# Expert loop of a mixture layer: gathers ahead of scatters, tables two chunks sooner, turned tiles one per chunk, bias rows alternating, spare rows from the last tile

## The chip, the cores and the metric

The kernel runs on one core of a Trainium2 chip (trn2). The metric is the device time of one execution in microseconds; less is better. The profile comes from one execution of the same program, recorded by the hardware profiler; its times count from the first instruction of the span.

## The reference, cut to what matters

One decoder layer over 512 tokens of width 1024. A mixing sublayer (pooling and short convolution, then an output projection) and a layer norm give `x1`. A mixture of 32 experts follows, of which each token uses 4. A second norm, a gated embedding and a third norm make the output.

```python
x = layer_norm(ALPHA * x + mix, ln1_g, ln1_b)
# for each expert e, on the rows that chose it:
gu = xb @ w_gate_up[e] + b_gate_up[e]
gate = minimum(gu[:, :1024], 7.0); up = clip(gu[:, 1024:], -7.0, 7.0)
y = ((up + 1.0) * gate * sigmoid(1.702 * gate)) @ w_down[e] + b_down[e]
# weighted by the token's softmaxed router logits and summed over its 4 experts
x = layer_norm(ALPHA * x + ffn, ln2_g, ln2_b)
x = layer_norm(ALPHA * x + sigmoid(x @ ple_gate_w + ple_gate_b) * (p @ ple_proj), ln3_g, ln3_b)
```

## The kernel before, in words

**Precision.** Every float32 matrix is divided into a high part (rounded by a copy on ScalarE, L114) and a low part (the rest, a subtraction on VectorE, L117, called the split here); a product is three matrix products, `mm3`, L210 to L212. Weights are streamed once, in chunks of 1 MB, through a ring of buffers: `load` (L102), `split`, and `ahead(j)`, which gives a used chunk's buffers back and splits what is due three to five chunks ahead.

**First part.** The input projection and the mixers fill `y`. `project(i)` multiplies token tile i (128 tokens) by the output weights, 48 products; `norm(i)` adds the residual in `x1[i]` on VectorE (`piece`, L274), takes a power on GpSimd (L291), and scales (L296, L298). `x1[i]` is loaded from `x` by GpSimd's DMA (L509). Both `x1d` (rows to gather) and `acc` (rows to scatter-add into) are written from it (L551). `acc` has 96 spare rows behind the 512, into which an expert's unused places scatter; L518 fills them once with finite numbers, from rows of a tile of `x1` before the norm overwrites it. `turn(i)` transposes the normed tile on TensorE (L307) for the router; `turn(0)` stands three products into `project(2)`.

**Expert loop (L897).** Each expert has 96 places for rows (a loop at the end handles any more). In the order of the program, expert e does:
1. four bias products of 64 rows (L903), the two halves of gate on the array's rows 0 to 63, the two of up on 64 to 127;
2. eight chunks of gate/up weights, k = 0 to 7, each 12 products, then `ahead`. At k = 2 the hidden rows of expert e - 1 are transposed (`split_t`, L307, L322, L323). In even experts (and in expert 1) `tables` makes for two experts the lists of rows and their weights: at k = 1 and 2 a one-hot table on VectorE (L614), at k = 6 eight narrow products (L640) and their decoding (L621 to L628);
3. the transposition of the rows gathered for expert e + 1;
4. `act`: L335 on VectorE, L338 on ScalarE, L339 on GpSimd, the sigmoid L344, the multiply L345 on GpSimd, L347 on VectorE;
5. the down projection of expert e - 1, four chunks j = 0 to 3, with the multiply L345 queued behind j = 0 and L347 behind j = 2, then `emit`: L354 scales on ScalarE and L355 scatters on GpSimd (a DMA that adds);
6. `gather_next`: an indirect DMA on GpSimd (L313) fetches the rows of expert e + 2 into the buffer that the sigmoid has left.

All transpositions and tables share two PSUM banks (`tr`), taken in turn; a bank is free when its result has been read. Expert 0 has no down projection; it also holds `weigh` and, after k = 5, the transposition for expert 1 (TURN1). Expert 5 runs `further` (lists for experts with more than 96 rows). Expert 19 (EMBED + 1) runs `embed_parts`: four tiles of `p` are transposed (L841) and divided (L843), one at each of k = 2 to 5. Expert 31 runs `prepare`: the four gate tables are transposed (L893) all at k = 2. The order on every queue is the order of the program text (`manual_schedule`).

Of the kernel before, what the change touches and what calls it, by code (L numbers as in the profile page):

```python
# [21 lines left out]
S = 512  # L22
NT = S // P
D = 1024
ND = D // P
E = 32
TOPK = 4
F = 1024
CAP = 96
# [19 lines left out]
def tile_layer(ctx: ExitStack, tc: tile.TileContext, x, p, w_in, pool_mix, pool_scale, conv_w, w_out,  # L49
               ln1_g, ln1_b, router_w, router_b, w_gate_up, b_gate_up, w_down, b_down,  # L50
               ln2_g, ln2_b, ple_proj, ple_gate_w, ple_gate_b, ln3_g, ln3_b, out):
    nc = tc.nc
# [8 lines left out]
    def at(name, b, dtype, n=2048, offset=0):  # L61

        return nc.alloc_sbuf_tensor_at(name, [P, n], dtype, offset=base0 + 8192 * b + 4 * offset).ap()
# [4 lines left out]
    acc = dram.tile([S + CAP, D], F32, name="acc")  # L68

    def big(n=P):  # L70
        return ps.tile([n, 2, 512], F32, tag="big", name="big", bufs=3)

    def tr(shape):
        return ps.tile(shape, F32, tag="tr", name="tr", bufs=2)
# [75 lines left out]
    def done(j, queue=nc.sync):  # L150

        give(*owned.pop(j))
        used[0] = j + 1
        fill(queue)
# [11 lines left out]
    def ahead(j):  # L166
        done(j)
        splits()
# [39 lines left out]
    def mm3(o, ah, al, bh, bl, start, stop):  # L208

        nc.tensor.matmul(o, ah, bl, start=start, stop=False)  # L210
        nc.tensor.matmul(o, al, bh, start=False, stop=False)  # L211
        nc.tensor.matmul(o, ah, bh, start=False, stop=stop)  # L212
# [98 lines left out]
    def gather(e):  # L311
        xg = mp2.tile([P, F], F32, tag="sg", name="xg")[:CAP]
        nc.gpsimd.indirect_dma_start(out=xg, out_offset=None, in_=x1d,  # L313
                                     in_offset=bass.IndirectOffsetOnAxis(ap=idxg[:, e:e + 1], axis=0))
        return xg
# [10 lines left out]
    def split_t(src, tag, pool, bufs):  # L326
        both, put = two_parts(tag, pool, bufs)
        transposed(src, CAP, put)
        return both
# [19 lines left out]
    def emit(o, gate, idx, y, halves=False):  # L349
        if halves:  # L350
            nc.scalar.activation(y[:, :512], o[:, 0], AF.Copy, scale=gate)
            nc.vector.tensor_scalar(y[:, 512:], o[:, 1], gate, None, op0=ALU.mult)
        else:
            nc.scalar.activation(y, o.rearrange("p a b -> p (a b)"), AF.Copy, scale=gate)  # L354
        nc.gpsimd.indirect_dma_start(out=acc, out_offset=bass.IndirectOffsetOnAxis(ap=idx, axis=0), in_=y,  # L355
                                     in_offset=None, compute_op=ALU.add)
# [9 lines left out]
    with tc.tile_pool(name="mix", bufs=1, side=RIGHT) as q:  # L366
# [112 lines left out]
        for j, cs in zip(order_in, c_in):  # L479
            o = o1 if len(cs) == 2 else big()  # L480
# [22 lines left out]
    x1 = [mp2.tile([P, D], F32, tag=n, name="x1") for n in ("gm", "h")]  # L503
# [11 lines left out]
        nc.scalar.dma_start(braw[32 * k:32 * k + 32], b_gate_up[0, :, (k // 2) * F:(k // 2 + 1) * F])  # L515
    nc.scalar.dma_start(rw, router_w[0].rearrange("(k p) e -> p k e", p=P))
    nc.scalar.dma_start(rb, router_b.to_broadcast([P, E]))
    nc.gpsimd.dma_start(acc[S:, :], x1[0][:CAP])  # L518
    lv = cp.tile([P, NT, E + 8], F32, name="lv")
    gsp = cp.tile([P, NT, 3, E], F32R, name="gsp")  # L520
    m8 = cp.tile([P, NT, 2, 8], F32, name="m8")
# [337 lines left out]
    def down(e, after={}, before={}):  # L859
        ah, al = hT.pop(e)  # L860
        o = big(CAP)
        for j in range(4):
            wh, wl = parts.pop(c_dn[e][j])
            for n in range(2):
                ns = slice(n * 512, (n + 1) * 512)
                for b in range(2):
                    k = 2 * j + b
                    mm3(o[:, n], ah[:, k], al[:, k], wh[:, b, ns], wl[:, b, ns], k == 0, k == ND - 1)
            for f in before.get(j, ()):
                f()  # L870
            if e == E - 2 and j == 2:
                done(c_dn[e][j])
            elif e < E - 1 or j < 3:
                ahead(c_dn[e][j])
            for f in after.get(j, ()):
                f()
        emit(o, gs[:, e:e + 1], idxs[:, e:e + 1], yos[e % 2][:CAP], e == E - 1)
        if e == E - 1:
            done(c_dn[e][-1])
# [6 lines left out]
    def prepare():  # L886

        nc.scalar.copy(bd, b3[:96])
        nc.vector.tensor_sub(bd[64:], b3[64:96], bd[64:].bitcast(F32))
        yield  # L890
        for i in range(NT):
            gt = tr([96, P])
            nc.tensor.transpose(gt, gsp[:, i].rearrange("p a b -> p (a b)").bitcast(F32), ident)  # L893
            nc.scalar.copy(gt_[:96, i * P:(i + 1) * P], gt)

    steps = iter(())
    for e in range(E):  # L897
        ah, al = xT.pop(e)
        gp, up = big(CAP), big(CAP)
        halves = [(gp, 0, 0), (gp, 1, 512), (up, 0, 1024), (up, 1, 1536)]  # L900
        for o, n, c in halves:
            r = slice(64 * (c // F), 64 * (c // F) + 64)
            nc.tensor.matmul(o[:, n], sel[r, e:e + 1].to_broadcast([64, CAP]), bsp[r, c % F:c % F + 512],  # L903
                             start=True, stop=False)
        for k in range(ND):
            wh, wl = parts.pop(c_gu[e][k])
            for o, n, c in halves:
                cs = slice(c, c + 512)
                mm3(o[:, n], ah[:, k], al[:, k], wh[:, 0, cs], wl[:, 0, cs], False, k == ND - 1)
            if k < ND - 1 or e:  # L910
                ahead(c_gu[e][k])
            if e == 0 and k == 0:
                next(first1, None)
                xg[1] = gather(1)
            if e == 0 and k == 1:
                weigh()
            if e == 0 and k == TURN1:
                xT[1] = split_t(xg.pop(1), "x", mp1, 1)
            if e and k == 2:
                hT[e - 1] = split_t(hs.pop(e - 1), "h", mp2, 1)  # L920
            if k == 1:
                steps = (tables(2, mp1) if e == 0 else tables(0, mp1) if e == 1 else
                         tables(e + 2, mp1) if e % 2 == 0 and e + 2 < E else
                         further() if e == 5 else prepare() if e == E - 1 else iter(()))
            if k in (1, 2, 6):
                next(steps, None)
            if e == EMBED + 1:
                if k == 1:
                    embed_steps = embed_parts()
                if 1 <= k <= 6:  # L930
                    next(embed_steps, None)
        last = e == E - 1
        if e and not last:
            xT[e + 1] = split_t(xg.pop(e + 1), "x", mp1, 1)
        steps_h = act(gp, up, lambda n: mp2.tile([P, F], F32, tag=n, name=n)[:CAP], nc.vector if last else nc.gpsimd)
        hs[e] = next(steps_h)
        if not last:
            next(steps_h)
        if e == 0:
            ahead(c_gu[0][-1])  # L940

        def multiply(steps_h=steps_h):
            next(steps_h)

        def gather_next(e=e):
            if e + 2 < E:
                xg[e + 2] = gather(e + 2)

        def finish(steps_h=steps_h):
            next(steps_h, None)  # L950

        if last:
            down(e - 1, {0: [finish, finish, finish]}, {3: [last_turn]})
            limit[0] = len(chunks)
            fill(nc.gpsimd)
        elif e:
            down(e - 1, {0: [multiply], 2: [finish]})
            gather_next()
        else:
            multiply()  # L960
            gather_next()
            finish()
        if e == EMBED - 1:

            spare_tiles = [more2.tile([P, 2, D], F32, tag=f"m{k}", name="after") for k in range(4)]
            ple = [t[:, k] for t in spare_tiles[:2] for k in range(2)]
            g2, b2 = spare_tiles[2][:, 0], spare_tiles[2][:, 1]
            pt, graw = spare_tiles[3][:, 0].rearrange("p (a b) -> p a b", a=NT), spare_tiles[3][:64, 1]
            assert len(late) == NT - 2 and len(extra) == 4
            pgb = at("pgb", RING + 1, F32R, D)[:64]  # L970
            ph, pl = (at(f"p{k}", RING + 2, F32R, D, k * D).rearrange("p (i k t) -> p i k t", i=NT, k=2) for k in range(2))
            nc.gpsimd.memset(graw, 0.0)
            nc.gpsimd.dma_start(pt, p[0, 0].rearrange("(i p) c -> p i c", p=P))

            for h in (0, 32):
                nc.gpsimd.dma_start(graw[h:h + 1], ple_gate_b)
            nc.gpsimd.dma_start(g2, ln2_g.to_broadcast([P, D]))
            nc.gpsimd.dma_start(b2, ln2_b.to_broadcast([P, D]))
        if e == EMBED + 1:
            embed()  # L980
            g3, b3 = spare_tiles[3][:, 0], spare_tiles[3][:, 1]
            gt_ = at("gt", RING + 2, F32R, S)
            bd = at("bd", RING + 1, F32R, D, D)[:96]

            for k in range(3):
                nc.gpsimd.dma_start(b3[32 * k:32 * k + 32], b_down[0])
# [124 lines left out]
```

## Time and profile before

| | |
|---|---|
| median of 3 runs | 1450.96 us (1449.4 to 1452.47) |
| the profiled execution | 1454.03 us |
| its span, mean granted clock | 1452.2 us, 0.989 |
| ScalarE busy | 952.4 us, 66% |
| GpSimd busy | 521.1 us, 36% |
| moved by DMA | 464.43 MB, mean 320 GB/s |

In the rows further down, PE is TensorE's products, PEld its weight loads, DVE is VectorE, ACT ScalarE, POOL GpSimd. A row names the line, the operation, what is written from what, and in brackets how long the engine stood idle just before and what ended that ("issue": nothing that the profile shows). The granted clock is the share of 2.4 GHz that TensorE got.

### The profile page before, as it was taken

The page shows a single profiled execution, that of the slowest core. Times are in us where ns is not written, and L with a number is a line of the kernel's source. Part 1 is how long each engine was busy: PE and PEld are TensorE (multiplying, and loading weights), DVE is VectorE, ACT ScalarE, POOL GpSimd, SP SyncE. Part 2 cuts the span into 40 slices and gives each one's busy share as a digit, 9 for nine tenths or more (in the row PEclk, how much of TensorE's full clock was granted, in tenths as well). Part 3 has the DMA queues.
Part 4 walks back from the last instruction along what each step waited for, and adds up shares of the span by engine and source line. Part 5 has one row for each costly group of instructions (what it writes and reads, how often), then busy time and mean ns, then how long its engine had stood idle before and what let it go on. Part 6 is the DMA issues. An engine that isn't in the chain of part 4 may idle for free. (4 is left out here: it accounts for less than half of the span.)

```text
span 1452.2 us, 17680 instructions
## 1 busy us (share of the span) xinstructions
PE 1404.6 (97%) x6630; PEld 1003.2 (69%) x6630; DVE 1236.7 (85%) x1049; ACT 952.4 (66%) x741; POOL 521.1 (36%) x203
## 2 busy tenths in 40 slices
PE   9999999999999999999999998999999999998896
PEld 8787766766666666767666666766666666665575
DVE  7645589999999999999989997799999999997785
ACT  5321267777777777777777776677777777776631
POOL 1101025455345555555543351134343434331100
PEclk9999999999999999999999999999999999999998
DMA  9326889999999999999889999899999999998321
GB/s 332 110 88 219 330 327 340 384 376 365 366 375 374 364 371 353 377 362 354 318 281 373 361 397 336 298 346 385 365 382 358 381 364 377 370 378 302 108 102 44
DMA packets 98071, 464.43 MB, mean 320 GB/s; under 512 B 9424, under 2 KB 19168, under 8 KB 65216
## 3 DMA queue, kind: packets, MB, share of 16 engines
q1 hardware_dynamic: 86240, 426.02, 76.7%
q0 software_dynamic: 10080, 35.53, 9.8%
q10 hardware_dynamic: 1664, 1.72, 0.5%
q8 instruction: 54, 0.88, 0.2%
q14 instruction: 33, 0.27, 0.1%
HBM read 443.97 MB, written 19.27 MB: 319 GB/s over the span
## 5 line engine op out<-in xcount | busy, mean ns | idle before, releaser
L355 POOL DMA_INDIRECT acc<-yo,idxs x32 | 200.9, 6277 | 187.1 <-ACT yo L354 181.8
L339 POOL TENSOR_SCALAR h<-h 96x1024 f32<-96x1024 f32 x31 | 40.9, 1318 | 428.4 <-ACT h L338 428.4
L212 PE MATMUL big<-chunk,xh 128*96 128x512 f32 x480 | 189.1, 394 | 0.0
L211 PE MATMUL big<-chunk,xl 128*96 128x512 f32 x480 | 189.0, 394 | 0.0
L313 POOL DMA_INDIRECT xg<-x1d,idxg x31 | 142.4, 4595 | 22.8 <-DVE idxg L653 13.7
L345 POOL TENSOR_TENSOR gm<-gm,sg 96x1024 f32<-96x1024 f32 x31 | 103.5, 3337 | 66.4 <-ACT sg L344 64.0
L211 PE MATMUL big<-chunk,hl 128*96 128x512 f32 x268 | 106.2, 396 | 0.0
L212 PE MATMUL big<-chunk,hh 128*96 128x512 f32 x268 | 105.6, 394 | 0.0
L212 PEld LDWEIGHTS big<-chunk,xh 128*96 128x96 f32 x480 | 77.5, 161 | 33.1
L211 PEld LDWEIGHTS big<-chunk,xl 128*96 128x96 f32 x480 | 77.7, 162 | 30.6
L212 PEld LDWEIGHTS big<-chunk,hh 128*96 128x96 f32 x268 | 43.4, 162 | 19.0
L211 PEld LDWEIGHTS big<-chunk,hl 128*96 128x96 f32 x268 | 43.3, 162 | 17.6
L322 ACT CAST xh<-tr 128x384 fp32r<-128x384 f32 x64 | 27.4, 478 | 34.8 <-PE tr L307 34.8
L291 POOL TENSOR_TENSOR mv<-mv,mhalf 128x1 f32<-128x1 f32 x12 | 7.9, 655 | 109.5 <-DVE mv L290 97.8
L344 ACT ACTIVATE sg<-gm 96x1024 f32<-96x1024 f32 x32 | 34.0, 1062 | 16.2 <-DVE gm L335 9.4
L117 DVE TENSOR_TENSOR ring2dt.float32r<-ring2dt.float,ring13dt.float32r 128x2048 fp32r<-128x2048 f32 x14 | 34.7, 2482 | 9.4 <-ACT ring13dt.float32r L114 9.4
L354 ACT ACTIVATE yo<-big,gs 96x1024 f32<-96x1024 f32 x31 | 34.4, 1110 | 10.8 <-PE big L212 10.8
L347 DVE SCALAR_TENSOR_TENSOR h<-h,gm 96x1024 f32<-96x1024 f32 x32 | 38.8, 1211 | 2.6 <-POOL gm L345 2.6
L117 DVE TENSOR_TENSOR ring5dt.float32r<-ring5dt.float,ring3dt.float32r 128x2048 fp32r<-128x2048 f32 x13 | 31.1, 2392 | 11.0 <-ACT ring3dt.float32r L114 11.0
L117 DVE TENSOR_TENSOR ring12dt.float32r<-ring12dt.float,ring6dt.float32r 128x2048 fp32r<-128x2048 f32 x14 | 32.6, 2327 | 8.4 <-ACT ring6dt.float32r L114 8.4
L335 DVE TENSOR_SCALAR gm<-big 96x1024 f32<-96x1024 f32 x32 | 38.7, 1211 | 0.0
L117 DVE TENSOR_TENSOR ring10dt.float32r<-ring10dt.float,ring12dt.float32r 128x2048 fp32r<-128x2048 f32 x14 | 34.7, 2482 | 4.4 <-ACT ring12dt.float32r L114 4.2
(577 smaller groups left out, 4474.2 us busy)
## 6 DMA issues: line engine op xcount, KB each, us to landing
ring10dt.float<-in_w_gate_up_dram SPq DMA_DIRECT2D x18, 1024.0 KB, 6.7
ring2dt.float<-in_w_gate_up_dram SPq DMA_DIRECT2D x18, 1024.0 KB, 7.5
ring3dt.float<-in_w_gate_up_dram SPq DMA_DIRECT2D x18, 1024.0 KB, 7.6
ring4dt.float<-in_w_gate_up_dram SPq DMA_DIRECT2D x18, 1024.0 KB, 7.5
ring9dt.float<-in_w_gate_up_dram SPq DMA_DIRECT2D x18, 1024.0 KB, 8.0
ring13dt.float<-in_w_gate_up_dram SPq DMA_DIRECT2D x17, 1024.0 KB, 6.8
ring1dt.float<-in_w_gate_up_dram SPq DMA_DIRECT2D x17, 1024.0 KB, 6.5
ring5dt.float<-in_w_gate_up_dram SPq DMA_DIRECT2D x17, 1024.0 KB, 6.9
```

The lines of the kernel that those rows point to most:

```text
L117: second()
L211: nc.tensor.matmul(o, al, bh, start=False, stop=False)
L212: nc.tensor.matmul(o, ah, bh, start=False, stop=stop)
L313: nc.gpsimd.indirect_dma_start(out=xg, out_offset=None, in_=x1d, in_offset=bass.IndirectOffsetOnAxis(ap=idxg[:, e:e + 1], axis=0))
L322: nc.scalar.copy(hi[:, 4 * h:4 * h + 4], t)
L335: nc.vector.tensor_scalar(gm, gp, LIMIT, None, op0=ALU.min)
L339: mul.tensor_scalar(h, h, LIMIT, -LIMIT, op0=ALU.min, op1=ALU.max)
L344: nc.scalar.activation(sg, gm, AF.Sigmoid, scale=SW_ALPHA)
L345: mul.tensor_mul(gm, gm, sg)
L347: nc.vector.scalar_tensor_tensor(h, h, 1.0, gm, op0=ALU.add, op1=ALU.mult)
L354: nc.scalar.activation(y, o.rearrange("p a b -> p (a b)"), AF.Copy, scale=gate)
L355: nc.gpsimd.indirect_dma_start(out=acc, out_offset=bass.IndirectOffsetOnAxis(ap=idx, axis=0), in_=y, in_offset=None, compute_op=ALU.add)
```

## The change

The spare rows are filled from tile 3 in place of tile 0. `prepare` yields before each tile, so that it does one tile per step. The bias products go gate half 0, up half 0, gate half 1, up half 1. The third step of `tables` and `further` runs at k = 4 in place of 6; the steps of `prepare` run at k = 1, 3, 4, 5, 6, and those of `embed_parts` too, in place of 1 to 6 (of which the last had nothing left to do). From expert 1 on the gather for expert e + 2 is queued behind chunk j = 1 of the down projection, ahead of the scatter.

```diff
--- before.py
+++ after.py
@@ -515,7 +515,7 @@
         nc.scalar.dma_start(braw[32 * k:32 * k + 32], b_gate_up[0, :, (k // 2) * F:(k // 2 + 1) * F])
     nc.scalar.dma_start(rw, router_w[0].rearrange("(k p) e -> p k e", p=P))
     nc.scalar.dma_start(rb, router_b.to_broadcast([P, E]))
-    nc.gpsimd.dma_start(acc[S:, :], x1[0][:CAP])
+    nc.gpsimd.dma_start(acc[S:, :], x1[NT - 1][:CAP])
     lv = cp.tile([P, NT, E + 8], F32, name="lv")
     gsp = cp.tile([P, NT, 3, E], F32R, name="gsp")
     m8 = cp.tile([P, NT, 2, 8], F32, name="m8")
@@ -887,8 +887,8 @@
 
         nc.scalar.copy(bd, b3[:96])
         nc.vector.tensor_sub(bd[64:], b3[64:96], bd[64:].bitcast(F32))
-        yield
         for i in range(NT):
+            yield
             gt = tr([96, P])
             nc.tensor.transpose(gt, gsp[:, i].rearrange("p a b -> p (a b)").bitcast(F32), ident)
             nc.scalar.copy(gt_[:96, i * P:(i + 1) * P], gt)
@@ -898,7 +898,7 @@
         ah, al = xT.pop(e)
         gp, up = big(CAP), big(CAP)
         halves = [(gp, 0, 0), (gp, 1, 512), (up, 0, 1024), (up, 1, 1536)]
-        for o, n, c in halves:
+        for o, n, c in halves[::2] + halves[1::2]:
             r = slice(64 * (c // F), 64 * (c // F) + 64)
             nc.tensor.matmul(o[:, n], sel[r, e:e + 1].to_broadcast([64, CAP]), bsp[r, c % F:c % F + 512],
                              start=True, stop=False)
@@ -922,12 +922,12 @@
                 steps = (tables(2, mp1) if e == 0 else tables(0, mp1) if e == 1 else
                          tables(e + 2, mp1) if e % 2 == 0 and e + 2 < E else
                          further() if e == 5 else prepare() if e == E - 1 else iter(()))
-            if k in (1, 2, 6):
+            if k in ((1, 2, 4) if e < E - 1 else (1, 3, 4, 5, 6)):
                 next(steps, None)
             if e == EMBED + 1:
                 if k == 1:
                     embed_steps = embed_parts()
-                if 1 <= k <= 6:
+                if k in (1, 3, 4, 5, 6):
                     next(embed_steps, None)
         last = e == E - 1
         if e and not last:
@@ -954,8 +954,7 @@
             limit[0] = len(chunks)
             fill(nc.gpsimd)
         elif e:
-            down(e - 1, {0: [multiply], 2: [finish]})
-            gather_next()
+            down(e - 1, {0: [multiply], 1: [gather_next], 2: [finish]})
         else:
             multiply()
             gather_next()
```

## Rows read from the trace of the kernel before

**Rows 1.** page, first part: busy us (share of span) and instructions by engine

```profile
PE 1404.6 (97%) x6630; PEld 1003.2 (69%) x6630; DVE 1236.7 (85%) x1049; ACT 952.4 (66%) x741; POOL 521.1 (36%) x203
```

**Rows 2.** TensorE's waits: us in total, times, longest

```profile
PE tr L307 <- DMA xg<-x1d,idxg: 6.5, 6, 1.8
PE tr L893 <- DVE hl L323: 4.8, 1, 4.8
...
PE tr L307 <- DVE tabsb L621: 3.0, 8, 0.4
```

**Rows 3.** timeline of TensorE near 133: start, us, what, idle before

```profile
133.25 1.94 PE L307 MATMUL tr<-ident,x 128*128 128x128 f32 x8 [2.91 <-issue]
```

**Rows 4.** table by stretch: us, busy by engine, granted clock, DMA share, GB/s

```profile
133.25:136.30 3.05, 3.04 (x12) 2.76 (x13) 2.99 (x3) 1.17 (x2) 1.12 (x2) 0.50 0.56 226
...
876.20:880.80 4.60, 4.58 (x12) 3.21 (x13) 0.85 (x2) 0.37 (x1) 0.00 (x0) 0.51 1.02 308
...
1327.90:1331.20 3.30, 3.27 (x9) 1.91 (x10) 0.38 (x1) 1.05 (x4) 0.00 (x0) 0.50 0.26 103
558.20:560.00 1.80, 0.08 (x1) 0.00 (x0) 1.72 (x1) 0.00 (x0) 0.00 (x0) 1.00 1.00 344
```

**Rows 5.** timeline of TensorE in experts 19, 21 and 22

```profile
870.90 0.82 PE L307 MATMUL tr<-ident,h 96*128 96x96 f32 x8
...
876.22 0.69 PE L841 MATMUL tr<-ident,after 128*128 128x128 f32 x2 [4.49 <-DVE hl L323]
...
989.65 0.47 PE L210 MATMUL big<-ring10dt.float32r,xh 128*96 128x512 f32 x1
...
998.06 0.82 PE L307 MATMUL tr<-ident,h 96*128 96x96 f32 x8
...
1004.26 0.40 PE L210 MATMUL big<-ring9dt.float32r,xh 128*96 128x512 f32 x1
...
1013.90 0.55 PE L307 MATMUL tr<-ident,xg 96*128 96x96 f32 x4 [0.40 <-DVE tabsb L621]
```

**Rows 6.** timeline of VectorE near 128

```profile
128.00 0.69 DVE L274 SCALAR_TENSOR_TENSOR x<-x,big 128x512 f32<-128x512 f32 x1 [12.46 <-DMA acc<-x]
```

**Rows 7.** DMA issues from 112.9 to 113.2: count, KB each, us to landing

```profile
early<-in_x_dram POOLq DMA_DIRECT2D x1, 512.0 KB, 12.4
```

**Rows 8.** timeline of GpSimd from 40 to 182

```profile
114.28 0.53 POOL L518 DMA_DIRECT2D acc<-x  x1 [0.93 <-DMA x<-in_x_dram]
...
131.25 1.00 POOL L291 TENSOR_TENSOR mv<-mv,mhalf 128x1 f32<-128x1 f32 x1 [16.25 <-DVE mv L290]
```

**Rows 9.** timeline of GpSimd in experts 14 and 21

```profile
681.59 11.37 POOL L355 DMA_INDIRECT acc<-yo,idxs  x1 [4.77 <-ACT yo L354]
693.26 4.97 POOL L313 DMA_INDIRECT xg<-x1d,idxg  x1 [0.30 <-DVE oh L614]
...
984.21 3.24 POOL L345 TENSOR_TENSOR gm<-gm,sg 96x1024 f32<-96x1024 f32 x1 [2.38 <-ACT sg L344]
```

**Rows 10.** timeline of TensorE in expert 14

```profile
705.91 0.85 PE L307 MATMUL tr<-ident,xg 96*128 96x96 f32 x8 [1.69 <-DMA xg<-x1d,idxg]
```

**Rows 11.** timeline of VectorE in experts 14, 21 and 22

```profile
686.63 2.28 DVE L117 TENSOR_TENSOR ring9dt.float32r<-ring9dt.float,chunk 128x2048 fp32r<-128x2048 f32 x1
...
985.95 3.65 DVE L117 TENSOR_TENSOR ring10dt.float32r<-ring10dt.float,ring12dt.float32r 128x2048 fp32r<-128x2048 f32 x1 [0.77 <-ACT ring12dt.float32r L114]
...
1003.07 0.55 DVE L614 TENSOR_TENSOR oh<-iota,rk 128x384 bf16<-128x384 f32 x1
...
1013.69 0.16 DVE L621 COPY tabsb<-tr 96x12 f32<-96x12 f32 x1
```

**Rows 12.** timeline of TensorE in expert 0

```profile
203.46 0.48 PE L640 MATMUL tr<-aux,oh 128*96 128x6 bf16 x8 [0.59 <-DVE xl L323]
```

**Rows 13.** timeline of TensorE at the start of expert 5

```profile
353.19 0.47 PE L903 MATMUL big<-bsp,sel 64*96 64x512 f32 x2
...
353.49 0.40 PE L903 MATMUL big<-bsp,sel 64*96 64x512 f32 x2
```

## The prediction

> **What bounds the kernel now.** The profiled execution took 1454.03 us, its span 1452.2. The page's first part shows TensorE busy for 97% of the span [rows 1], so time can be saved only where its products are fewer, closer together, or wait less. The list of TensorE's waits comes next [rows 2]. The reader is to see how little there is: three lines sum to 14.3 us, and two more stalls stand in the timeline, 2.91 us before 133.25 [rows 3] and 4.49 before 876.22 [rows 5]; this change touches each of them. The table by stretch gives the second half of the price [rows 4]: after the idles of 2.91, 4.49 and 4.76 us the granted clock is 0.50 or 0.51 (1.2 of 2.4 GHz) for 3.05, 4.60 and 3.30 us, while the stretch after an idle of 1.77 us inside 558.20 to 560.00 is still at 1.00. Half of a stretch at 0.50 is lost. One more piece of arithmetic: a product's record lasts 0.40 us but the next begins 0.23 us after it (two chunks of twelve and a transposition lie between 998.06 and 1004.26 [rows 5]: 6.20 less 0.6, over 24). An idle is counted from a record's end, so the delay is the idle plus 0.17.
>
> **Spare rows.** VectorE's first normalisation step waits 12.46 us for the store of tile 0 into the spare rows, because it overwrites that tile [rows 6]. Reading the last tile removes this wait. In its place GpSimd, which issues the store, must wait for the last tile: that load lands 12.4 us after its issue just before 112.9 [rows 7], so at about 125.2. Behind the store on GpSimd stand two memsets and the power of the same normalisation. The store's issue took 0.53 us, the memsets some 0.3, so the power starts at about 126.0 instead of 131.25 [rows 8]. VectorE needs 3.25 us from its first step to the power (128.00 to 131.25); the product it reads ended near 118.6 (the next one, 48 times 0.23 us, ends just before the transpositions are due), so it is ready by 122. The transpositions began 2.0 us after the power's start, so now at 128.0; TensorE arrives at 130.3 (133.25 less 2.91). Cover: 2.3 us. Gain 2.91 + 0.17 + 1.5 (half of 3.05) = **4.5**; ends 0 (load 5 us later) and 4.7.
>
> **Gather ahead of scatter.** In experts 1 to 29 GpSimd runs the multiply, idles for the scaled result (4.77 us before 681.59), issues the scatter (11.37) and only then the gather (4.97) [rows 9]. The gather lands at about 705.8 and TensorE has waited 1.69 us [rows 10]; this happens 6 times for 6.5 us [rows 2]. Moved behind chunk 1 of the down projection, the gather starts where the multiply ends, at 676.8, 16 us sooner; even with the longest issue, 11.4, it lands well before 704. The scatter now stands behind it. The two together need what they need today, begun 4.77 us earlier, so the clamp of the next expert, next on that queue, is not delayed; the scatter's own source alternates between two buffers and is wanted two experts later. Bytes and number of transfers are the same. Gain 6.5 + 6 x 0.17 = **7.5**; ends 6 and 7.5.
>
> **Tables at chunk 4 instead of 6.** Eight narrow products and seven small VectorE operations move ahead of two chunks. Now the copy out of the table's bank runs at 1013.69 behind a split [rows 11], and the expert's own transpositions wait 0.40 us for the bank [rows 5]; 8 times, 3.0 us [rows 2], with 0.17 each 4.4. Two chunks (5.6 us) more cover it. What is late next is the split before the next expert: after odd experts its first weight product already starts just when a 3.65 us split ends (985.95 + 3.65, against 989.65 [rows 5, 11]), and even experts come to the same place 0.57 us sooner. I give back 0.15 in seven of them. The moved products need the second one-hot table, finished at 1003.07 + 0.55 = 1003.62; they are due at 1004.26: no wait, by 0.6 us. Gain 4.4 - 1.1 = **3.3**; ends 0 and 4.4.
>
> **Turned tiles one per chunk.** In experts 19 and 31 they need a transposition bank that VectorE frees late: idles of 4.49 and 4.76 us [rows 2, 5], then 4.60 and 3.30 us at half clock [rows 4]. With record ends that is 4.6 + 2.3 = 6.9 and 4.8 + 1.7 = 6.5, plus 0.2 for four transpositions in a row in the second. After the change a chunk of 2.8 us stands in between. In expert 19 TensorE is done with the first transpositions at 871.5 (870.90 + 0.6), comes to the bank at 874.3, and the bank is free at 876.2 as now: about 1.95 us remain, likewise in expert 31. The row nearest to 1.95 is the idle of 1.77 without a drop, so I take no drop; the other end is about 2 us more in each. In expert 19 the last tile moves to chunk 6, where its bank is freed some 4 us later as with the tables, against 3 us until the gathered tile wants it: 1.0. Gain 6.9 - 2.95 + 6.7 - 1.95 = **8.7**; ends 4.7 and 13.6.
>
> **Experts 0 and 1.** The wait of 0.59 us before the tables in expert 0 goes [rows 12]: 0.8. But there VectorE is more than a chunk behind: the copy out of the bank comes behind a split, and expert 1's transpositions, right after chunk 5, want that bank; I take 1.0, between 0 and one split (2.28). In expert 1 the one-hot is about 0.4 late. Together **-0.6**; ends -2 and +0.8.
>
> **Bias products.** Their order alternates between the array's two row halves. In the trace of every expert from 2 on the four already start as two pairs, two at 353.19 and two at 353.49 [rows 13], so nothing is left to pair: **0**. Losing the pairing would cost two steps of 0.3 us in 30 experts, +18; that needs a reason which I don't see. The Trainium skill (TensorE: Matmul & The Clock Gate, Part 2) says that only weight loads are pulled ahead and "the MATMULs themselves stay in program order". By that the old order could overlap only its middle two, three steps instead of the two which the trace shows; the measurement decides.
>
> **Sum.** 4.5 + 7.5 + 3.3 + 8.7 - 0.6 = 23.4 us, from 1454.03 to 1430.6. The median of the three runs, 1450.96, lies 3.1 below that execution, so the forecast is **1427.6**.
>
> **Rivals.** (a) *The waits come back as late splits.* For: VectorE is busy 85% of the span [rows 1], and a row shows a split that ends as it is needed [rows 11]. Against: its idle gaps remain in the down projections. Then the tables give nothing and half of the gather's gain goes: 23.4 - 3.3 - 3.8 = 16.3, so 1434.7. (b) *The alternation does pay*, one step of 0.31 us in 30 experts, 9.3: 1418.3. Against it: the pairs. This is what the rule just quoted would give. (c) *The spare rows only change who waits*: the last tile lands so late that the power is no earlier; without the 4.5, 1432.1. (d) *Slower.* The gather's issue now lies beside the splits of the down projection. A multiply on GpSimd (984.21) stretched the split beside it from 2.28 to 3.65 us [rows 9, 11], 1.37 more, and from expert 16 on there is no slack at the first weight product. If the gather did the same to two splits in each of 14 experts, 14 x 2.74 = 38.4 less 23.4 would make it 15.0 slower: 1466.0 as median. It decides from 23.4 / 14 = 1.7 us per expert. Against: beside a scatter's issue splits took 2.28 [rows 11]; the issue itself stretched, to 11.37. The Trainium skill (GPSIMD Engine Reference, section 1) lists GpSimd's SBUF interfaces as shared with VectorE, with contention where an instruction has two SBUF inputs, as the split has. For the multiply the trace agrees; for the issue of a scatter it is GpSimd alone that pays.
>
> **How the numbers follow.** Forecast 0.70, (a) 0.14, (b) 0.05, (c) 0.05, (d) 0.05, unchanged within the bound 0.01. The bound is 0.2%, 2.9 us, about what a measurement of this kernel can tell from no change. The forecast's own range is 1424 to 1432; the range of 8 in 10 takes in (a), (c), and a dropped clock in experts 19 and 31, and reaches down to turned tiles with little left to wait: 1422 to 1436. Faster 0.94, same 0.01, slower 0.05.
>
> **What would show it.** In the list of TensorE's waits the line for the gather is gone, the tables' line nearly so; the lines for the turned tiles show about 2 us each and the granted clock stays at 1.00 there and at 130 to 137. GpSimd's rows run multiply, gather, scatter. The bias products still start in pairs. It is wrong if the turned tiles wait 4 us or more, if splits beside a gather take over 3 us, if the first weight products after odd and even experts wait over 0.5 us, or if the transpositions near 130 still wait.

## The result, and the profile after

The changed kernel takes 1431.80 us (median of 4 runs, 1430.62 to 1432.50), the kernel before beside it 1451.72 (4 runs); the ratio is 0.9855, interval 0.984 to 0.9869. Forecast were 1427.6, range 1422 to 1436: faster, by 19.9 us where 23.4 were summed up from a median of three runs (1450.96). The profiled execution took 1432.01, its span 1430.2.

First part of the page after (busy us, share, instructions), then four lines of TensorE's list of waits (total, times, longest):

```profile
PE 1396.6 (98%) x6630; PEld 998.2 (70%) x6630; DVE 1235.9 (86%) x1049; ACT 950.5 (66%) x741; POOL 446.9 (31%) x203
```

```profile
PE tr L893 <- DVE hl L323: 2.0, 1, 2.0
PE tr L841 <- DVE hl L323: 2.0, 1, 2.0
...
PE tr L307 <- DVE p L843: 0.9, 1, 0.9
...
PE tr L307 <- DVE tabsb L621: 0.7, 1, 0.7
```

Against [rows 1, 2] the line for the gathers is gone, the tables' line has one instance left (expert 0's), and the turned tiles wait 2.0 us each, as forecast. GpSimd is busy 74 us less.

**Spare rows.** VectorE (L274), GpSimd (L518, L291) and TensorE (L307), from the timelines after:

```profile
118.73 0.69 DVE L274 SCALAR_TENSOR_TENSOR x<-x,big 128x512 f32<-128x512 f32 x1 [3.27 <-PE big L212]
```

```profile
125.48 0.54 POOL L518 DMA_DIRECT2D acc<-early  x1 [12.23 <-DMA early<-in_x_dram]
...
126.15 0.59 POOL L291 TENSOR_TENSOR mv<-mv,mhalf 128x1 f32<-128x1 f32 x1
```

```profile
130.10 1.03 PE L307 MATMUL tr<-ident,x 128*128 128x128 f32 x8
```

The first norm step starts as its product ends (118.73 for 118.6 worked out), the power at 126.15 (126.0), and the transposition has no idle time in its bracket, where [rows 3, 6, 8] had 2.91 and 12.46 us. Expert 0 begins 4.77 us sooner than in the first profile (4.5).

**Gathers.** GpSimd and VectorE at the end of expert 13, the step of [rows 9, 11], and where TensorE uses the gathered rows ([rows 10]):

```profile
662.04 3.55 POOL L345 TENSOR_TENSOR gm<-gm,sg 96x1024 f32<-96x1024 f32 x1 [1.70 <-ACT sg L344]
665.87 2.74 POOL L313 DMA_INDIRECT xg<-x1d,idxg  x1 [0.27 <-POOL gm L345]
670.31 11.39 POOL L355 DMA_INDIRECT acc<-yo,idxs  x1 [1.70 <-ACT yo L354]
```

```profile
663.79 3.96 DVE L117 TENSOR_TENSOR ring3dt.float32r<-ring3dt.float,chunk 128x2048 fp32r<-128x2048 f32 x1 [0.46 <-ACT chunk L114]
667.67 2.28 DVE L117 TENSOR_TENSOR ring15dt.float32r<-ring15dt.float,chunk 128x2048 fp32r<-128x2048 f32 x1
```

```profile
692.75 0.82 PE L307 MATMUL tr<-ident,xg 96*128 96x96 f32 x8
```

Multiply, gather, scatter, as the change says; the gather is issued 26.9 us before its rows are used (12.65 before the change), without a wait. The split behind it takes 2.28 us: only the one beside the multiply is stretched, as before (3.95 us in the same step there, with no gather beside it). In the whole profile 33 splits lie beside a gather's issue and not beside the multiply, and each took 2.28 us. VectorE's busy time fell by 0.8 us [rows 1]; rival (d) would have added some 38.

**Tables.** VectorE in expert 22 after, one-hot and copy out of the bank, and TensorE's narrow products and the transposition of the gathered rows:

```profile
985.85 0.54 DVE L614 TENSOR_TENSOR oh<-iota,rk 128x384 bf16<-128x384 f32 x1
...
990.94 0.16 DVE L621 COPY tabsb<-tr 96x12 f32<-96x12 f32 x1
```

```profile
987.05 0.48 PE L640 MATMUL tr<-aux,oh 128*96 128x6 bf16 x8
...
995.77 0.82 PE L307 MATMUL tr<-ident,xg 96*128 96x96 f32 x8
```

The one-hot ends 0.66 us ahead of the products (0.6 worked out), and the copy is done at 991.10, 4.7 us before the transposition, whose eight products now run without a stop; in [rows 5, 11] the second four waited 0.40 us for it.

**Turned tiles.** TensorE after in expert 19, and the table by stretch (us, busy by engine, granted clock, DMA share, GB/s) behind the idles of experts 19 and 31:

```profile
862.42 0.44 PE L841 MATMUL tr<-ident,after 128*128 128x128 f32 x2 [1.97 <-DVE hl L323]
...
877.38 0.55 PE L307 MATMUL tr<-ident,xg 96*128 96x96 f32 x4 [0.86 <-DVE p L843]
```

```profile
863.50:866.70 3.20, 3.20 (x9) 2.02 (x8) 1.86 (x2) 0.17 (x1) 0.00 (x0) 0.50 1.02 429
...
1309.70:1313.00 3.30, 3.30 (x17) 2.30 (x16) 1.69 (x1) 1.56 (x1) 0.00 (x0) 1.00 0.86 343
```

The idles are those forecast (1.95), and so is L307's wait for the last tile: 0.86 + 0.17 = 1.03 (1.0). But in expert 19 the granted clock fell to 0.50 for some 3.2 us (9 products there, 17 in expert 31 in about the same time), which the sum had excluded.

### The profile page after: what moved, and what is told of

Read it like the earlier page. It is cut to its first block, busy times and chain, and to the rows that moved or that the text cites. A ratio compares the mean times of both kernels' runs of the same rounds, so it can differ in the third digit from the quotient of the medians.

```text
span 1430.2 us, 17695 instructions
## 1 busy us (share of the span) xinstructions
PE 1396.6 (98%) x6630; PEld 998.2 (70%) x6630; DVE 1235.9 (86%) x1049; ACT 950.5 (66%) x741; POOL 446.9 (31%) x203
## 4 chain that ended last, share of the span: by engine, by line
PE 87%; DVE 6%; issue 4%; DMA 1%; ACT 1%; POOL 0%; SPq 0%; DVEq 0%; ACTq 0%; POOLq 0%
PE big L210 26%; PE big L212 25%; PE big L211 25%; PE tr L307 4%; PE big L1038 3%; DVE ring7dt.float32r L117 1%; PE big L903 1%; DVE ring8dt.float32r L117 1%; DVE ring10dt.float32r L117 1%; DVE ring6dt.float32r L117 1%; DVE ring2dt.float32r L117 1%; DMA acc<-yo,idxs 0%; PE big L206 0%; DMA x<-acc 0%; PE tr L569 0%
## 5 line engine op out<-in xcount | busy, mean ns | idle before, releaser
L355 POOL DMA_INDIRECT acc<-yo,idxs x32 | 177.5, 5547 | 92.3 <-ACT yo L354 87.0
L313 POOL DMA_INDIRECT xg<-x1d,idxg x31 | 91.7, 2958 | 21.9 <-DVE idxg L653 13.7
L354 ACT ACTIVATE yo<-big,gs 96x1024 f32<-96x1024 f32 x31 | 34.4, 1110 | 10.9 <-PE big L212 10.9
L117 DVE TENSOR_TENSOR ring5dt.float32r<-ring5dt.float,ring3dt.float32r 128x2048 fp32r<-128x2048 f32 x13 | 31.1, 2390 | 11.4 <-ACT ring3dt.float32r L114 11.4
L117 DVE TENSOR_TENSOR ring8dt.float32r<-ring8dt.float,ring11dt.float32r 128x2048 fp32r<-128x2048 f32 x14 | 34.7, 2478 | 6.1 <-ACT ring11dt.float32r L114 6.1
L322 ACT CAST hh<-tr 128x384 fp32r<-128x384 f32 x62 | 26.5, 479 | 16.8 <-PE tr L307 16.8
```

The costliest lines, as they stand in the source:

```text
L117: second()
L322: nc.scalar.copy(hi[:, 4 * h:4 * h + 4], t)
```

## The experiments

Each part was undone by itself in the changed kernel, or made by itself in the kernel before; times are medians, and those beside which a kernel ran are named. The table below is worked out from the profiled executions: how long each stage took, from the first bias product of one expert to that of another ("end" is TensorE's last product).

```
                        to e0   e0-e2   e2-e16  e16-e19 e19-e20 e20-e31 e31-end
before                 180.72   64.10   508.50   108.56   55.01  396.18  127.60
before_again           178.11   64.09   509.46   108.57   54.37  396.28  129.34
only_spare             176.18   64.12   509.55   108.55   54.50  396.22  128.65
only_gather_tables     176.96   64.25   500.00   107.54   54.79  393.84  128.29
only_turned            177.46   64.15   507.57   108.58   50.43  396.20  125.81
no_gather              175.97   64.23   506.56   107.52   52.53  393.87  124.36
no_tables              176.23   64.12   500.83   108.54   50.54  395.87  125.11
no_turned              176.38   64.24   499.90   107.52   55.01  393.86  127.82
no_spare               176.75   64.22   499.90   107.52   50.89  393.88  124.41
no_spare_again         177.05   64.25   499.90   107.55   50.93  393.82  123.10
no_bias                175.87   64.22   500.00   107.53   50.92  393.88  124.53
after                  175.95   64.24   499.90   107.52   52.51  393.86  124.67
after_again            175.63   64.24   499.90   107.53   50.91  393.87  123.78
better                 175.57   64.23   499.99   107.52   49.21  393.84  120.92
```

**after_again**: the changed kernel, unaltered.

> The changed kernel once more, unaltered: a second profiled execution of it, and times beside the other runs on this chip. Theory: 1431.8 us within 1 us; in expert 19 (860 to 870 us) TensorE waits 1.97 us for the transposition banks and its granted clock falls to 0.50 for some 3 us behind that wait, while behind the like wait in expert 31 (1307 to 1309 us) it stays at 1.00; the idle time ahead of the second acc load (L1011) is 7 to 8 us. Rival: the fall of the clock in expert 19 and the longer landing of the last scatter belong to the one execution that was profiled; then the clock stays at 1.00 in both experts, the final wait is about 7.1 us, and the profiled execution is 1.5 to 3 us shorter.

Measured: 1430.78 us (5 runs, 1428.82 to 1432.40; before 1453.01; ratio 0.9848, 0.9832 to 0.9865). The idle of 1.97 us in expert 19 is there, and this time the clock stayed at 1.00 behind it (the stretch that answers to 863.50:866.70):

```profile
863.20:866.40 3.20, 3.20 (x17) 2.28 (x16) 1.84 (x2) 1.52 (x1) 0.00 (x0) 1.00 1.03 435
```

So the fall is not fixed to this idle; expert 19 took 1.60 us less. The final wait was 7.2 us against 7.9. The rival was right on all three counts.

**no_gather**: the gather behind the scatter again.

```diff
-            down(e - 1, {0: [multiply], 1: [gather_next], 2: [finish]})
+            down(e - 1, {0: [multiply], 2: [finish]})
+            gather_next()
```

> The gather goes back behind the scatter; all the rest of the change stays. Theory (the gather is worth 7.5 us, all of it between experts 4 and 16 and at the later even experts): 1439.3 us, 1438.3 to 1440.5; the xg waits of TensorE come back with 6 instances and about 6.5 us, and GpSimd issues L313 behind L355 again. Rival 1: of the 8.6 us that the experts 2 to 16 gained, some came from a shorter cadence that has nothing to do with the gather; then 1436 to 1437.5. Rival 2: a gather issued among the splits stretches them in the changed kernel, so that undoing it gives some of its cost back: under 1436.

Measured: 1437.96 us (4 runs, 1436.12 to 1438.89; ratio to before 0.9894, 0.9875 to 0.9913), 7.2 over after_again. TensorE's waits, and GpSimd in expert 13:

```profile
PE tr L307 <- DMA xg<-x1d,idxg: 5.5, 5, 1.6
```

```profile
675.13 11.42 POOL L355 DMA_INDIRECT acc<-yo,idxs  x1 [4.71 <-ACT yo L354]
686.86 4.97 POOL L313 DMA_INDIRECT xg<-x1d,idxg  x1 [0.30 <-DVE oh L614]
```

The old order and the old waits are back; the loss lies in the column e2-e16 (6.66 over the changed kernel; expert 19's 52.53 is that of an execution with the fall, as in the profile after), as forecast. The time is just under the theory's range (1438.3) and over rival 1's (1437.5). Rival 2 falls.

**no_tables**: the third step at chunk 6 again.

```diff
-            if k in ((1, 2, 4) if e < E - 1 else (1, 3, 4, 5, 6)):
+            if k in ((1, 2, 6) if e < E - 1 else (1, 3, 4, 5, 6)):
```

> The tables' last step goes back from chunk 4 to chunk 6 of the product; all the rest of the change stays. Theory: 3.1 us lost, 1434.9 us (1434.2 to 1435.7); the tabsb waits come back at the even experts from 16 with 0.4 us each, and the starts of the odd experts behind them lose their 0.12 us wait for L117. Rival: the wait for tabsb is replaced by another that ends at the same time (the split behind it): 1431.8 to 1432.5.

Measured: 1433.60 us (4 runs, 1432.81 to 1434.61; ratio 0.9865, 0.9847 to 0.9883), 2.8 over after_again where 3.1 were expected, and under the theory's range (1434.2). The rival falls: the wait is back as it was:

```profile
PE tr L307 <- DVE tabsb L621: 3.0, 8, 0.4
```

Columns e16-e19 and e20-e31 grow by 1.02 and 2.01, e2-e16 by 0.93, and expert 19's falls by 0.37. The column e0-e2 loses 0.12: the small price in experts 0 and 1 belongs to this part.

**no_turned**: the turned tiles in their old places (tiles of 19 at chunks 2 to 5, of 31 all at chunk 2).

```diff
+        yield
         for i in range(NT):
-            yield
...
-            if k in ((1, 2, 4) if e < E - 1 else (1, 3, 4, 5, 6)):
+            if k in ((1, 2, 4) if e < E - 1 else (1, 2, 6)):
...
-                if k in (1, 3, 4, 5, 6):
+                if 1 <= k <= 6:
```

> The turned tiles of experts 19 and 31 go back to the places they had before (in 19 tiles at chunks 2 to 5, in 31 all four at chunk 2); all the rest of the change stays. Theory: 7.2 us lost (2.5 in expert 19, 4.7 in expert 31), 1439.0 us (1438 to 1440); expert 19's bias products to expert 20's are 2.5 us further apart than in the changed kernel, expert 31 ends 4.7 us later. Rival: the fall of the clock in expert 19 of the changed kernel was that execution's alone, and the turned tiles are worth 4.0 + 4.7 = 8.7 us as predicted: 1440.5 us.

Measured: 1438.01 us (4 runs, 1437.79 to 1438.14; ratio 0.9897, 0.9879 to 0.9914), 7.2 over after_again. Both waits are 4.8 us again; expert 19's column grows by 4.1 over an execution without the fall and 2.5 over one with it, e31-end by 4.0 over after_again. By median that is the theory's number, with other shares than its 2.5 and 4.7 us: against the means of all executions with the tiles one per chunk (51.45 where the tables are early too, and 124.47), it is 3.6 in expert 19 and 3.4 in expert 31.

**no_spare**: the spare rows from tile 0 again.

```diff
-    nc.gpsimd.dma_start(acc[S:, :], x1[NT - 1][:CAP])
+    nc.gpsimd.dma_start(acc[S:, :], x1[0][:CAP])
```

> The spare rows of acc are filled from tile 0 of x again; all the rest of the change stays. Theory: 4.8 us lost in the prologue and kept to the end, 1436.6 us (1435.8 to 1437.4); TensorE waits 2.9 us at 133 us and its granted clock is 0.50 for some 3 us behind it, and every later expert starts 4.8 us later. Rival: the prologue's loss is taken back by waits for transfers further on (the weights or the acc loads of the tail are the bound): 1431.8 to 1434.

Measured: 1431.24 us (5 runs, 1429.55 to 1433.42; before 1452.14; ratio 0.9855, 0.9832 to 0.9878): no loss that can be measured. Theory and rival both fall. VectorE waits for the store again, but TensorE hardly does; VectorE's and TensorE's timelines, then the table by stretch:

```profile
125.39 0.69 DVE L274 SCALAR_TENSOR_TENSOR x<-x,big 128x512 f32<-128x512 f32 x1 [10.31 <-DMA acc<-x]
```

```profile
130.64 1.27 PE L307 MATMUL tr<-ident,x 128*128 128x128 f32 x8 [0.76 <-issue]
```

```profile
133.00:137.00 4.00, 4.00 (x26) 3.18 (x25) 3.83 (x8) 0.25 (x1) 0.02 (x1) 1.00 0.73 297
...
1308.90:1312.20 3.30, 3.30 (x10) 2.20 (x9) 1.68 (x1) 0.34 (x1) 0.00 (x0) 0.52 0.84 341
```

The store landed 11.4 us after its issue instead of 13.6, the idle was 0.76, and no half clock followed. The last row shows something else: here it is expert 31, whose clock had held in the profile after, that fell to 0.52.

**no_bias**: the four bias products in the old order.

```diff
-        for o, n, c in halves[::2] + halves[1::2]:
+        for o, n, c in halves:
```

> The four bias products go back to the order gate, gate, up, up; all the rest of the change stays. Theory: no difference, 1431.8 us within 0.8 us; the four products start as two pairs whose halves are 4 ns apart, as in both kernels so far. Rival: by program order the first two products run one behind the other on the same rows, and the alternation saves 0.3 us in each of 31 experts: 1441 us.

Measured: 1431.10 us (5 runs, 1430.31 to 1431.58; ratio 0.9854, 0.9832 to 0.9876). Expert 5's bias products and the first weight product, in the changed kernel and in this one:

```profile
347.32 0.70 PE L903 MATMUL big<-bsp,sel 64*96 64x512 f32 x4
347.95 0.47 PE L210 MATMUL big<-ring9dt.float32r,xh 128*96 128x512 f32 x1
```

```profile
347.25 0.70 PE L903 MATMUL big<-bsp,sel 64*96 64x512 f32 x4
347.88 0.48 PE L210 MATMUL big<-ring9dt.float32r,xh 128*96 128x512 f32 x1
```

Four products in 0.63 us in either order. Two in the same 64 rows start 0.3 us apart, so the order gate, gate, up, up would need three such steps, 0.9 us. The Trainium skill (TensorE: Matmul & The Clock Gate, Part 2) says that matmuls stay in program order; here the trace does not agree: products on different row halves run as pairs whichever way they are written. The rows don't name the halves; that a pair is one of each follows from expert 0, where two of one half start 0.31 us apart (180.72 and 181.02 in the kernel before). There a product that waits does hold up the one behind it: in the changed kernel the second waits until 176.73, and the third, whose half was free some 0.5 us sooner, starts with it and not before.

**before_again, no_spare_again, only_spare** settle what the spare rows are worth: the first two are unaltered, the third is the kernel before with this one part.

```diff
-    nc.gpsimd.dma_start(acc[S:, :], x1[0][:CAP])
+    nc.gpsimd.dma_start(acc[S:, :], x1[NT - 1][:CAP])
```

> The kernel before once more, unaltered, for a second profiled execution of it. Theory A (the price of the spare rows is a transfer's landing, which varies between executions of the same kernel, with the fall of the clock on top of it once the wait is long enough): the 384 KB transfer acc<-x lands 11 to 14 us after its issue, TensorE waits 0.7 to 3 us ahead of turn(0) at about 130 us, its clock stays at 1.00 where that wait is under 2 us, and expert 0 starts between 177 and 181 us. Theory B (what differs is fixed in each kernel): 13.6 us to landing, 2.9 us of idle time, clock at 0.50, expert 0 at 180.7 us, as in the first profile.

> The changed kernel with the spare rows filled from tile 0 again, unaltered against the first time: a second profiled execution of it. Theory A (the landing varies between executions): the transfer acc<-x lands 11 to 14 us after its issue, expert 0 starts between 176.5 and 181 us, and the time is 1430 to 1435 us. Theory B (what differs is fixed in each kernel): 11.4 us to landing, 0.8 us of idle time, no half clock, expert 0 at 176.8 us.

> The kernel before with one part of the change alone: the spare rows are filled from tile 3 of x instead of tile 0. Theory A (the price varies between executions from 1 to 4.8 us): 1 to 4 us under the kernel before's median, and VectorE no longer waits for acc<-x. Theory B (the kernel before has the long wait and the half clock in all its executions): 4.8 us under it, within 1 us. Rival: the profiled execution of the kernel before was a rare one, and the gain is under 1 us.

Measured: before_again 1453.61 and no_spare_again 1429.97 us (one time each), only_spare 1452.28 (12 runs, 1450.72 to 1458.95) against 1452.42 (17 runs; ratio 1.0006, 0.9992 to 1.002). The second execution of the kernel before, TensorE and the DMA issues from 60 to 135:

```profile
132.01 1.27 PE L307 MATMUL tr<-ident,x 128*128 128x128 f32 x8 [1.51 <-issue]
```

```profile
acc<-x POOLq DMA_DIRECT2D x1, 384.0 KB, 11.2
```

For the landing Theory A holds by before_again (11.2 us, expert 0 at 178.11); no_spare_again, with 11.1 us and 177.05, fits both theories. With tile 0 the idle was 2.91, 1.51, 0.76, 0.69, 0.50 and 0.93 us in six executions, and only the first, the one that was read for the prediction, brought the half clock. The column "to e0" has 176.75 to 180.72 for tile 0 and 175.57 to 176.38 for tile 3: means 177.84 and 175.97, worth 1.9 us, 1.3 without the extreme. The medians show even less (0.1 both ways), and only_spare's interval allows a gain of at most 1.2 us. So for its time both theories fall (1 to 4 us, 4.8 us), and the rival, under 1 us, fits best. Whether a gain of some 1 us is there isn't settled; nor is whether the two longest, both of the kernel before, are chance, nor why the landing varies.

**only_gather_tables, only_turned**: parts alone in the kernel before. The sum of the parts undone singly is 7.2 + 2.8 + 7.2 + 0.1 for the spare rows (1431.24 against no_bias) + 0 = 17.3, and the whole is 19.9 to 22.2.

```diff
-            if k in (1, 2, 6):
+            if k in ((1, 2, 4) if e < E - 1 else (1, 2, 6)):
...
-            down(e - 1, {0: [multiply], 2: [finish]})
-            gather_next()
+            down(e - 1, {0: [multiply], 1: [gather_next], 2: [finish]})
```

> The kernel before with two parts of the change alone: the gather ahead of the scatter and the tables' last step at chunk 4. Undone singly in the changed kernel they cost 7.2 and 2.8 us, all five parts singly 17.8 us, against 21 to 22 us for the whole change. Theory A (the two overlap: with both in their old places the waits for the gathers are longer): together they are worth 12 to 14 us here, 1438.5 to 1440.5 us against the kernel before's 1452.4. Theory B (they add up, and the remainder lies elsewhere): 10 us, 1442.4 us, within 1 us. In both the waits for xg are gone, and in the profile expert 16 starts 565 to 566 us behind expert 0 (before: 572.6 and 573.6).

The other moves the tiles as the change does, and leaves the tables' third step at 6.

> The kernel before with one part of the change alone: the turned tiles of experts 19 and 31 one in a chunk. Theory A: 7.2 us as when it is undone in the changed kernel, 1445.2 us (1444 to 1446.5), between 2.5 us in expert 19 where the clock falls and 4.0 us where it doesn't, and 4 us in expert 31. Theory B (the remainder lies here: behind the late gathers of the kernel before the turned tiles cost more): 9 to 11 us, 1441.5 to 1443.5 us.

Measured: only_gather_tables 1440.99 us (6 runs, 1439.04 to 1442.03; ratio 0.9908, 0.9886 to 0.993), only_turned 1443.64 (6 runs, 1440.70 to 1445.83; ratio 0.9926, 0.9902 to 0.9949), before 1452.93: 11.9 and 9.3 us. With the spare rows' 0.1 that is 21.3, about the whole. only_turned lies where theory A ends and theory B begins, and its interval, 7.4 to 14.2 us, takes in both; its profiled execution has 4.3 us in expert 19 and 2.5 in e31-end, so some 2.5 of the 9.3 are not found in the stages that the tiles are in. For gather and tables the overlap shows in e2-e16: the gather is worth 6.66 where the tables are early (no_gather), but 7.9 where they are late (four executions at 507.57 to 509.55, mean 508.77, against no_tables' 500.83). Theory A's 12 to 14 was just missed, and an overlap of 1.3 us leaves the rest of the distance between the two sums, 2.7 us, to the spread of the medians; expert 16 starts 564.25 us behind expert 0, a little under what both theories gave.

The overlap is not only longer waiting. In two of the four executions with both parts in their old places, one late gather brought a half clock; in before_again, TensorE at the wait and the stretch behind it:

```profile
702.68 0.85 PE L307 MATMUL tr<-ident,xg 96*128 96x96 f32 x8 [1.78 <-DMA xg<-x1d,idxg]
```

```profile
703.50:706.90 3.40, 3.40 (x10) 2.19 (x9) 2.21 (x4) 3.40 (x5) 1.04 (x1) 0.50 1.04 411
```

In only_spare the like wait was 1.84 us before 700.83, with 0.51 from 701.90 to 705.30. These two have the longest e2-e16 of all (509.46 and 509.55). At some 1.6 us a fall, an estimate from expert 19, they make about 0.8 of the mean's 1.3 us. The gather's wait, too, ends in a transfer's landing and so is a sample: it totals 5.5 to 6.5 us in five executions with the old order.

**better**: a version built on what was found. Tiles 0 and 1 behind chunk 0, where both transposition banks are free, tile 2 behind chunk 4, tile 3 behind chunk 5, the copies of `pgb` and `bd` last.

```diff
...
+            if k == 0 and e in (EMBED + 1, E - 1):
+                turned = embed_parts() if e == EMBED + 1 else prepare()
+                next(turned)
+                next(turned)
+            if k in (1, 2, 4) and e < E - 1:
                 next(steps, None)
...
+            if k in (4, 5, 6) and e in (EMBED + 1, E - 1):
+                next(turned, None)
```

> The changed kernel with its turned tiles moved once more: in experts 19 and 31 tiles 0 and 1 are turned behind chunk 0's products, where both transposition banks are long free, tile 2 behind chunk 4, tile 3 behind chunk 5, and the copies of pgb and bd come last, behind chunk 6. Theory: the waits of 1.97 us (expert 19) and 1.99 us (expert 31) behind chunk 2's transposition go, with the half clock that follows the first (1.5 us) and the wait of L307 for L843 (1.03 us): 4.5 + 2.0 = 6.5 us saved, 1425.3 us (1424 to 1427). Rival 1: ScalarE and VectorE, given the tiles' copies at chunk 0, come later to chunk 2's transposition, and the wait stands there instead: 1430 to 1432. Rival 2: only the waits go and no half clock, since its fall was one execution's: 1426.8.

Measured: 1424.65 us (5 runs, 1423.98 to 1425.23; ratio to before 0.9807, 0.9785 to 0.9829), 6.5 below no_bias beside it: faster than both kernels. The theory's time came out, with other shares than its 4.5 and 2.0 us: no wait for L841's or L893's place is left, but expert 19 took 49.21 us, only 1.7 less than without the fall and 2.2 less than the mean. The rest of its gain stands in a new wait; TensorE at `embed`'s first product, and the split that it waits for:

```profile
885.43 0.47 PE L210 MATMUL big<-ring3dt.float32r,p 128*128 128x512 f32 x1 [1.46 <-issue]
```

```profile
881.69 3.64 DVE L117 TENSOR_TENSOR ring3dt.float32r<-ring3dt.float,ring10dt.float32r 128x2048 fp32r<-128x2048 f32 x1 [0.78 <-ACT ring10dt.float32r L114]
```

That split stands beside the multiply and ends at 885.33. In e31-end the gain is 3.55 on the mean of eight executions with the tiles one per chunk (124.47).

## Why the prediction was right, and where it was not

The direction and the mechanisms came out; the forecast was 3 to 4 us low. The sum was 1 to 3.5 us too large, and 1450.96, the median of three runs that it was taken from, lay 0.8 to 2.0 under the medians measured beside the changed kernel. By the means of the table's columns:

- **Spare rows, 4.5: the step that failed.** "Gain 2.91 + 0.17 + 1.5 (half of 3.05) = 4.5" is true of the one execution read (4.77); the columns' means give 1.9, and the times of whole runs at most 1.2. The stall ends in a transfer's landing, 13.6 us there and 10.9 to 11.5 in the five others; its size was a sample, and only there the half clock came on top. The range's lower end, 0, was given for another reason (a late load).
- **Part of the same stall was probably counted twice.** The step "lies 3.1 below that execution, so the forecast is 1427.6" carried the whole offset of the profiled execution over to the new kernel. Expert 0 began 3.4 us later in it than in the mean of the other five with tile 0 (177.27), so the offset may well have been this stall, which the change takes away; that is argued from the stages, not shown by a run. 23.4 less 2.6 (4.5 less 1.9) from 1450.96 would have been 1430.2.
- **Gathers 7.5 and tables 3.3**: together 10.8; measured 8.87 in e2-e16 (508.77 to 499.90) and 3.39 in e16-e19 and e20-e31, 12.26. They overlap by 1.3, which a sum of single terms can't show; some 0.8 of it is the half clock behind the longest gather waits, which the term (waits and 0.17 each) has at nothing and which the one execution read did not have. Rivals (a) and (d) are out: no late split took the gain, and no split was stretched.
- **Turned tiles 8.7**: waits as forecast, but "I take no drop" holds in only part of the executions. Expert 19 saves 3.8 us without the fall (54.74 on the mean of five to 50.91) and 2.2 with it, for 3.95; expert 31 on the mean 3.87 for 4.75. A fall costs 1.6 us.
- **Experts 0 and 1, -0.6**: -0.12. **Bias products, 0**: none; rival (b) is out. Rival (c) is out as it was put (the power did come sooner), though its time, 1432.1, is close to the one measured: little was to be had there in most executions.

By columns: 1.87 - 0.12 + 8.87 + 3.39 + 3.29 (expert 19, 54.74 to 51.45, the mean of the six executions with tables early and tiles one per chunk) + 3.87 = 21.2, between the two differences of medians, 19.9 and 22.2.

## What to carry to other kernels

A stall that ends in a transfer's landing is one sample: look for what it would be with a landing some us sooner, and don't both remove it at full size and carry the profiled execution's excess over to the median. Parts that relieve the same queue are tried both ways, undone singly and made singly: the two sums differed by 4 us here (17.3 and 21.3, for a whole of 19.9 to 22.2), and part of that showed where two parts relieve the same wait. Work that needs a shared bank goes where the bank has long been free, not one chunk later.

## What the runs showed of the hardware that was not expected

- After an idle of 1.95 to 1.99 us the granted clock fell in 6 of 14 cases (2 of 6 in expert 19, 4 of 8 in expert 31, told by the clock of the stretch behind, 0.50 to 0.52 against 1.00 in the rows above). In the expert loop it held after every idle of up to 1.77 us and fell after 1.78 and 1.84 (the late gathers of before_again and only_spare) and after 4.49 to 4.77; in the first part it held after 0.50 to 1.51 with tile 0 and fell after 2.91. So "the row nearest to 1.95 is the idle of 1.77 without a drop" took one outcome near a length at which both occur. That these falls make the times spread isn't shown: no_bias has both idles and spreads over 1.3 us, after_again and no_spare over 3.6 and 3.9, and the version `better`, without them, over 1.25.
- A gather's issue on GpSimd took 4.97 us behind the scatter and 2.74 ahead of it in the step shown; in the first profile the 31 gathers took 0.97 to 9.83 us, in the profile after 29 of the 31 took 2.71 to 2.77; over the kernel the gathers' issues sum to 142 us before and 92 after. The Trainium skill (GPSIMD Engine Reference, section 1) tells of SBUF interfaces shared by VectorE and GpSimd: for the multiply the rows agree (a split of 3.96 us beside it, 2.28 without), for the issues it is their own length that varies, and no run here tells why.
